# The FFN input projections of an encoder layer: block products of full depth, and seven half-depth products of block sums

## The chip, the cores and the metric

One core of a Trainium2 chip runs the kernel. The metric is the device time of one execution in microseconds (us), the median of the runs shown. The engines have short names here: PE is TensorE (matmul), PEld its weight load, DVE is VectorE, ACT is ScalarE, POOL is GpSimd and SP is SyncE, whose queue issues the DMAs. SBUF is the on-chip memory with 128 partitions, PSUM the accumulator memory of PE with eight banks of 128 x 512 float32.

## The reference, cut to what matters

The layer has 2048 tokens of width 1024. A normalised input goes through one projection, attention and a state-space mixer run side by side, an output projection is added to the residual, and then comes the FFN, which is all that the change touches. With hidden width 2816:

```python
h = rms_norm(x, norm2[i]) * (1.0 + sc2) + sh2
gt, up = jnp.split(h @ w_ffn_in[i], 2, axis=-1)
x = x + g2 * ((jax.nn.silu(gt) * up) @ w_ffn_out[i])
...
return rms_norm(x, final_norm)
```

## The kernel before

The program is written with tile pools. A scheduler puts the instructions of each engine in an order of its own, and each engine then follows its order: an instruction that waits holds up all that stands behind it on its engine. A pool gives a name a fixed number of buffers, and a new tile waits until its buffer has been read for the last time. All DMAs of the FFN stand in SP's queue, in one order too.

**Precision.** Every float32 operand of a large matmul is split in two parts of the fast type fp32r: `hi` is a cast (ACT), `lo` the operand minus `hi` (DVE or POOL). A product is three matmuls per 128 rows of depth: hi by hi, lo by hi, hi by lo.

**Stage 3** (`mix_tile`, `out_tile`, L989 to L1042) takes the tokens in 16 tiles of 128. `out_tile` makes the output projection in two PSUM halves, multiplies them by a gate into `tm` (DVE, L1025), adds them to the residual row tile `xt` (POOL, L1026), stores it to `x2_d` in DRAM, squares and sums it (ACT, L1030), and POOL makes the factor of the norm (L1032, L1033), a column of `rs2`, which stays in SBUF.

**FFN.** There are four blocks of 512 tokens. `ffn_prep(b)` (L1072) loads four row tiles `x2n`, scales them by `rs2` (ACT, L1079), transposes them on PE into PSUM tiles `ps_t4` (L1084), applies gain and shift (DVE, L1086, into `tf`), and splits the result into `ht` (ACT L1087, DVE or POOL L1088). `ffn_in` (L1091) takes the hidden columns in 22 steps f of 128. A step loads the gate's and the up half's weights [1024 x 128] (`weight`, L1062: DMA, ACT cast L1068, DVE or POOL difference L1069), and makes two sums of 24 matmuls of 128 x 128 by 128 x 512 (L1102), each in a PSUM bank of its own. Tanh (ACT) and two DVE operations that read PSUM give `th`, and ACT and POOL split it into `act`, which stays in SBUF (L1106 to L1110). `ffn_out` (L1113) makes one half of the output columns: 22 x 4 x 3 matmuls into the four banks `ps_f` (L1134 to L1136). It is called twice for a block, and the next block's `ffn_prep` stands between the two calls. `last_norm` (L1142) makes the final norm and stores the rows.

PSUM has separate pools there: two banks for the transposes, two for `ps_h`, four for `ps_f`, of which `ffn_in` borrows two in every other step.

Of the kernel before, what the change touches and what calls it, by code (L numbers as in the profile page):

```python
# [17 lines left out]
P = 128  # L18
D = 1024
# [29 lines left out]
W3A = 5  # L49
FH = 2816  # L50
# [14 lines left out]
def tile_encoder(ctx: ExitStack, tc: tile.TileContext, I, O, stop=None, dbg=None):  # L65
# [27 lines left out]
    x2_d = [dram([P, 4, D], f"x2_d{b}") for b in range(4)]  # L93
    bt_d = dram([NGC, P, GC * 2 * P], "bt_d")
# [54 lines left out]
    with ExitStack() as p1:  # L149
# [15 lines left out]
        # ---- tables of the SSM  # L165
# [26 lines left out]
        def expand(ch, eng=V):  # L192
            """state-in, state-out and in-chunk tables of GC groups"""
# [16 lines left out]
            # re: cre*are - cim*aim; minus im: ncim*are - cre*aim  # L210
# [19 lines left out]
            # impulse responses within a chunk; columns: forward only | backward only | both  # L230
# [25 lines left out]
        # ---- conditioning vector and the columns of the small parameters  # L256
# [18 lines left out]
        def row_of(i):  # L275
            """selects row i of nr for all partitions"""
# [4 lines left out]
        def ada_chunk(c0, w, tag="ad"):  # L281
            """columns c0 to c0 + w of c_act @ w_ada"""
# [70 lines left out]
        def modulate(tf, src, ht, ks, eng):  # L353
            """hi and lo parts of the modulated rows, transposed"""
# [15 lines left out]
        def ssm_setup():  # L370
            # ---- SSM parameters
# [16 lines left out]
            # dt = exp(log_dt)  # L388
# [6 lines left out]
            # exp(lr * dt) - 1 through tanh  # L395
# [7 lines left out]
            # angle reduced to [-pi, pi]  # L403
# [30 lines left out]
            # powers 0..8  # L434
# [12 lines left out]
            # unit rotor of 8 steps (backward: conjugate) and its doublings, renormalised; decay of 8 steps  # L447
# [10 lines left out]
            # directional power tables  # L458
# [8 lines left out]
            # the state input is turned back by one chunk: pbd = pb0 * e^{-i phi}, where phi is 8 steps  # L467
            # in the direction of time; un holds e^{i phi} forward and its conjugate backward
# [7 lines left out]
        def ssm_setup2(kre, kim):  # L476
# [21 lines left out]
            # Bbar = k * b  # L498
# [7 lines left out]
        # the first tiles advance with the weights  # L506
# [20 lines left out]
        def in_main(s, ht, ta, begun):  # L527
# [8 lines left out]
            def norm_rope(src, i, n):  # L536
                """heads of src, rotated, and their reciprocal norms"""
# [50 lines left out]
        def rotors(chunks, eng, tags):  # L588
            """e^{i phi m} over the half chunks"""
# [35 lines left out]
    # ------------------------------------------------------------------ attention and SSM  # L625
# [5 lines left out]
    with ExitStack() as p2:  # L631
# [30 lines left out]
        def prep_k(g, first):  # L662
            """keys as split parts: the high part of the first head, or the rest"""
# [15 lines left out]
        def prep_q(u):  # L679
            """queries of a block for a pair of heads, as split parts"""  # L680
# [20 lines left out]
        def prep_max(u):  # L701
            """minus the row maxima, as a row of the second operand"""
# [105 lines left out]
        def advance(u, n):  # L808
            """up to n steps of the preparation, not beyond unit u + 2; the steps of unit u before it starts"""
# [4 lines left out]
        def ssm_chunk(c):  # L814
            """GC groups"""
# [120 lines left out]
    # ------------------------------------------------------------------ GLU, output projection, residual  # L936
    rs2 = const([P, S], "rs2")
    with ExitStack() as p3:
# [33 lines left out]
        def split_t(src, n, dst):  # L972
            """transposes of [tokens, n * P] to hi and lo parts"""
# [15 lines left out]
        def mix_tile(s):  # L989
            """normalised mixer outputs of a tile, transposed and split"""  # L990
# [15 lines left out]
            # the SSM half is 4 times its value  # L1006
# [10 lines left out]
        def out_tile(s, mt):  # L1017
# [15 lines left out]
            GP.tensor_tensor(rs2[:, s:s + 1], r2, mhalf[:, 0:1], op=ALU.pow)  # L1033
# [15 lines left out]
    # ------------------------------------------------------------------ FFN  # L1049
    ps_h = ctx.enter_context(tc.tile_pool(name="ps_h", bufs=1, space=PSUM, reuse_waits="tile"))  # L1050
    ps_t = ctx.enter_context(tc.tile_pool(name="ps_t4", bufs=2, space=PSUM, reuse_waits="tile"))
    ps_f = ctx.enter_context(tc.tile_pool(name="ps_f", bufs=1, space=PSUM, reuse_waits="tile"))
    h4 = ctx.enter_context(tc.tile_pool(name="h4", bufs=1, reuse_waits="tile"))
    w4 = ctx.enter_context(tc.tile_pool(name="w4", bufs=3, reuse_waits="tile"))
    a4 = ctx.enter_context(tc.tile_pool(name="a4", bufs=1, reuse_waits="tile"))
    t4 = ctx.enter_context(tc.tile_pool(name="t4", bufs=2, reuse_waits="tile"))
    g2b = a4.tile([P, D], F32, tag="g2b", name="g2b")
    fnb = a4.tile([P, D], F32, tag="fnb", name="fnb")
# [3 lines left out]
    def weight(src, n, cnt):  # L1062
        """[P, n, m] of weights as hi and lo parts"""
        raw = w4.tile([P, n, src.shape[2]], F32, tag="raw", name="w_raw")
        dma(raw, src)
        hi = w4.tile([P, n, src.shape[2]], F32R, tag="whi", name="w_hi")
        lo = w4.tile([P, n, src.shape[2]], F32R, tag="wlo", name="w_lo")
        A.copy(hi, raw)  # L1068
        (GP if cnt % 4 == 3 else V).tensor_sub(lo, raw, hi)  # L1069
        return hi, lo  # L1070

    def ffn_prep(b):  # L1072
        """transposed, modulated rows of a block as hi and lo parts"""
        ht = h4.tile([P, 2, KD, 512], F32R, tag="ht4", name="ht4")
        xs = []
        for j in range(4):
            xt = h4.tile([P, D], F32, tag="x2n", name="x2n", bufs=4)
            dma(xt, x2_d[b][:, j, :])
            A.activation(xt, xt, AF.Copy, scale=rs2[:, 4 * b + j:4 * b + j + 1])  # L1079
            xs.append(xt)  # L1080
        for k in range(KD):
            pt = ps_t.tile([P, 512], F32, tag="t4", name="ps_t4")
            for j in range(4):
                T.transpose(pt[:, P * j:P * (j + 1)], xs[j][:, P * k:P * (k + 1)], ident)  # L1084
            tf = h4.tile([P, 512], F32, tag="tf", name="tf", bufs=2)
            V.tensor_scalar(tf, pt, gain2[:, k:k + 1], modc[:, 24 + k:25 + k], op0=MUL, op1=ADD)  # L1086
            A.copy(ht[:, 0, k], tf)  # L1087
            (GP if b == 0 and k % 2 else V).tensor_sub(ht[:, 1, k], tf, ht[:, 0, k])  # L1088
        return ht

    def ffn_in(ht):  # L1091
        act = [a4.tile([P, KF, 512], F32R, tag=f"act{i}", name=f"act{i}") for i in range(2)]
        for f in range(KF):
            ph = []
            for i, c0 in enumerate((P * f, FH + P * f)):
                hi, lo = weight(wfi[:, :, c0:c0 + P], KD, i)
# [113 lines left out]
```

## Time and profile before

| | |
|---|---|
| three runs | 3050.66, 3050.98, 3051.86 us, median 3050.98 |
| the profiled execution | span 3050.2 us |
| PE, DVE, POOL, ACT busy, share of the span | 95%, 52%, 42%, 38% |
| moved by DMA | 292.24 MB, mean 96 GB/s |
| the FFN in it | from 1583 us to the end |

The profiled execution's own time is its span, from the first to the last event that was recorded; it is 0.8 us below the median of the runs. A row of a view has the line of the program, the engine and the operation, what it writes and reads, and a duration in us or, where it says so, in ns. A PE row of a matmul lasts longer than the distance to the next one, since matmuls are pipelined. PEclk is the granted clock of TensorE: 1.00 is 2.4 GHz and 0.50 is 1.2 GHz, and a mean between them is a stretch with both.

### The profile page before, as it was taken

What the parts mean: (1) busy time and instruction counts of PE and PEld (TensorE: products, weight loads), DVE (VectorE), ACT (ScalarE), POOL (GpSimd) and SP (SyncE); (2) the same over time, 40 slices, a digit from 0 to 9 for tenths busy, and PEclk for the clock granted to TensorE, in tenths of its full rate; (3) what the DMA queues carried; (4) which work ended last, traced back from release to release, by engine and by line L of the source; (5) the groups of instructions that cost most, each with busy time, mean ns of one, the idle gap of its engine ahead of it and who ended that gap; (6) DMA issues with size and microseconds to landing.
All of it is one profiled execution on the core that took longest, in us unless ns stands there. A gap on an engine that the chain in (4) does not pass through costs nothing.

```text
span 3050.2 us, 36157 instructions
## 1 busy us (share of the span) xinstructions
PE 2901.0 (95%) x13548; PEld 2129.6 (70%) x13548; DVE 1598.9 (52%) x2271; ACT 1156.6 (38%) x2227; POOL 1279.9 (42%) x1062
## 2 busy tenths in 40 slices
PE   6998978889889999999999999999999999999998
PEld 4776835445445455458878888888888888888887
DVE  6879886777887755653343333433334332343323
ACT  3654544444444445452333222322223222232222
POOL 3647568778888977433231111211112111121112
PEclk7999998989999999999999999999999999999999
DMA  7764221111110100022254332533334332243322
GB/s 211 216 221 152 86 69 41 49 45 49 45 45 25 56 11 11 4 90 83 87 173 124 97 97 93 178 98 97 98 122 152 97 97 97 91 153 97 98 98 80
DMA packets 331648, 292.24 MB, mean 96 GB/s; under 512 B 44024, under 2 KB 278224, under 8 KB 330448
## 3 DMA queue, kind: packets, MB, share of 16 engines
q1 hardware_dynamic: 331472, 289.92, 30.0%
q8 instruction: 107, 1.75, 0.2%
q14 instruction: 69, 0.57, 0.1%
HBM read 243.24 MB, written 46.64 MB: 95 GB/s over the span
## 4 chain that ended last, share of the span: by engine, by line
PE 69%; DVE 4%; issue 1%; POOL 1%; ACT 1%; DVEq 0%; POOLq 0%; ACTq 0%
PE ps_h L1102 31%; PE ps_y L986 6%; PE ps_f L1134 5%; PE ps_f L1135 5%; PE ps_f L1136 5%; PE ps_o L770 4%; PE ps_st L784 2%; PE ps_s L712 2%; PE ps_st L785 2%; PE ps_z L986 2%; DVE xs L876 1%; DVE xs L875 1%; DVE mx L713 1%; DVE ys L128 1%; PE ps_t L977 1%
## 5 line engine op out<-in xcount | busy, mean ns | idle before, releaser
L1102 PE MATMUL ps_h<-ht,w_hi 128*128 128x512 f32 x2816 | 869.4, 390 | 2.3 <-DVE ht L1088 2.3
L1069 DVE TENSOR_TENSOR w_lo<-w_raw,w_hi 128x1024 fp32r<-128x1024 f32 x248 | 305.9, 1234 | 680.8 <-ACT w_hi L1068 680.6
L1068 ACT CAST w_hi<-w_raw 128x1024 fp32r<-128x1024 f32 x264 | 277.9, 1053 | 983.8 <-issue 628.8
L1102 PEld LDWEIGHTS ps_h<-ht,w_hi 128*128 128x128 f32 x2816 | 528.9, 188 | 112.2 <-DVE ht L1088 2.6
L1102 PE MATMUL ps_h<-ht,w_lo 128*128 128x512 f32 x1408 | 548.5, 390 | 0.4 <-DVE w_lo L1069 0.4
L1110 POOL TENSOR_TENSOR act<-th,act 128x512 fp32r<-128x512 f32 x88 | 157.1, 1786 | 775.9 <-ACT act L1109 775.9
L713 DVE TENSOR_REDUCE mx<-ps_s 128x1 f32<-128x512 f32 x512 | 333.1, 682 | 107.7 <-PE ps_s L712 105.6
L1102 PEld LDWEIGHTS ps_h<-ht,w_lo 128*128 128x128 f32 x1408 | 264.8, 188 | 55.8 <-DVE w_lo L1069 0.8
L1135 PE MATMUL ps_f<-w_hi,act 128*128 128x512 f32 x704 | 274.2, 389 | 0.0
L1136 PE MATMUL ps_f<-w_lo,act 128*128 128x512 f32 x704 | 273.9, 390 | 0.0
L1134 PE MATMUL ps_f<-w_hi,act 128*128 128x512 f32 x704 | 273.8, 390 | 0.0
L712 PE MATMUL ps_s<-ka,qa 128*128 128x512 f32 x512 | 211.6, 454 | 48.3 <-DVE mx L713 46.9
L368 PE MATMUL ps_z<-whi,ht 128*128 128x512 f32 (+1 forms) x768 | 226.9, 379 | 15.0 <-ACT ht L357 11.0
L784 PE MATMUL ps_st<-qa,ka 128*128 128x512 f32 x512 | 224.9, 439 | 14.9 <-ACT e__6941 L787 2.5
L712 PEld LDWEIGHTS ps_s<-ka,qa 128*128 128x128 f32 x512 | 93.6, 192 | 189.0 <-DVE mx L713 133.2
L785 PE MATMUL ps_st<-qb,kb 128*128 128x512 f32 x512 | 208.3, 407 | 0.1
L986 PE MATMUL ps_y<-wo,mt 128*128 128x512 f32 x768 | 186.2, 394 | 1.2 <-DVE on L751 0.9
L1108 DVE SCALAR_TENSOR_TENSOR th<-th,ps_h 128x512 f32<-128x512 f32 x88 | 60.5, 687 | 227.0 <-PE ps_h L1102 226.8
L368 PEld LDWEIGHTS ps_z<-whi,ht 128*128 128x128 f32 x768 | 141.1, 199 | 44.8 <-ACT ht L357 12.8
L784 PEld LDWEIGHTS ps_st<-qa,ka 128*128 128x128 f32 x512 | 98.9, 193 | 102.7 <-issue 21.7
L986 PEld LDWEIGHTS ps_y<-wo,mt 128*128 128x128 f32 x768 | 142.1, 188 | 35.3 <-DVE mt L980 4.7
L1135 PEld LDWEIGHTS ps_f<-w_hi,act 128*128 128x128 f32 x704 | 132.2, 188 | 27.3
(2266 smaller groups left out, 5041.5 us busy)
## 6 DMA issues: line engine op xcount, KB each, us to landing
w_raw<-in_w_ffn_in_dram SPq DMA_DIRECT2D x176, 512.0 KB
w_raw<-in_w_ffn_out_dram SPq DMA_DIRECT2D x88, 512.0 KB
wa<-in_w_ada_dram SPq DMA_DIRECT2D x48, 512.0 KB
xt<-in_x_dram SPq DMA_DIRECT2D x32, 512.0 KB
rot_d<-rot SPq DMA_DIRECT2D x16, 512.0 KB
rotl<-rot_d SPq DMA_DIRECT2D x8, 1024.0 KB
x_d<-xt SPq DMA_DIRECT2D x16, 512.0 KB
x2n<-x_d SPq DMA_DIRECT2D x16, 512.0 KB
```

The source lines that it names most:

```text
L368: T.matmul(pp[:, 0:c1 - c0], ht[:, a, k], w[:, k, c0:c1], start=k == 0 and j == 0, stop=k == KD - 1 and j == 2)
L712: T.matmul(p1_, qa[h][:, P * j:P * (j + 1)], ka[kv][f], start=True, stop=True)
L713: red = V.reduce_max(mx[:, 4 * h + j, f:f + 1], p1_, axis=AX.X)
L784: T.matmul(st_, ka[kv][k // 4][:, ks], qa[h], start=True, stop=False)
L785: T.matmul(st_, kb[kv][k // 4][:, ks], qb[h], start=False, stop=True)
L986: T.matmul(out, lhs[:, a, k], rhs[w][k][:, cs_], start=n == 0, stop=n == last)
L1068: A.copy(hi, raw)
L1069: (GP if cnt % 4 == 3 else V).tensor_sub(lo, raw, hi)
L1102: T.matmul(pp, w[:, k], ht[:, a, k], start=n == 0, stop=n == 23)
L1134: T.matmul(pf[j], act[0][:, f, js], hi[:, e], start=f == 0, stop=False)
L1135: T.matmul(pf[j], act[1][:, f, js], hi[:, e], start=False, stop=False)
L1136: T.matmul(pf[j], act[0][:, f, js], lo[:, e], start=False, stop=f == KF - 1)
```

## The change

Tokens are now taken in two halves of 1024. Depth (1024 rows of the weights) is cut in two halves of 512, the tokens of a half in two groups of 512, and the hidden columns of a step f in gate and up. That is a 2 x 2 by 2 x 2 block product, and it is made with seven block products of depth 512 in place of eight, by sums of blocks (`s1` and the like on the weights, `t1` to `t4_` on the activations). Sums and differences are made in float32 before the split in hi and lo.

- `out_tile` also scales its row tile by the norm's factor (`xn`, ACT) and stores it to DRAM (`xn_d`). `xn` takes the only buffer of the name `tm`.
- `ffn_prep(t)` handles a half in four parts kk. It loads two depth tiles of 128 as `xk` (one buffer), transposes them into four PSUM banks, and makes seven operands `xc0` to `xc6` [128 x 512], each with hi and lo. They stay in 28 buffers.
- `ffn_in(t, xc)` has 22 steps of seven products `prod` with 12 matmuls. Three banks `ps_ha`, `ps_hb`, `ps_hc` serve a step. A partial sum is copied out of the bank (`r1`, `r2`, `r3`, ACT) and the accumulation goes on in it. `th` is split and stored to DRAM (`act_d`).
- `ffn_out(b, last)` makes both halves of the columns at once in eight banks. It reads the activations back (`act_i`, 512 KB per f) into the buffers of `xc`, and the weights as two [128 x 512] tiles. `finish_rows` loads the residual rows, adds, normalises and stores.
- All eight PSUM banks are one name of one pool.

```diff
+NTMP = 10
+NHL = 14
+NRAW = 8
...
+            rs2 = t3.tile([P, 1], F32, tag="rs2", name="rs2")
+            GP.tensor_tensor(rs2, r2, mhalf[:, 0:1], op=ALU.pow)
+            xn = t3.tile([P, D], F32, tag="tm", name="xn", bufs=1)
+            A.activation(xn, xt, AF.Copy, scale=rs2)
+            dma(xn_d[s // 8][:, s % 8, :], xn)
...
+    def bank(name):
+        return ps_a.tile([P, 512], F32, tag="acc", name=name, bufs=8)
+    def slot(i, kk, name, dt=F32R):
+        return xc4.tile([P, 2, 512], dt, tag=f"xc{i}{kk}", name=name)
+    def split(src, eng):
+        hi, lo = half("w_hi"), half("w_lo")
+        A.copy(hi, src)
+        eng.tensor_sub(lo, src, hi)
...
+    def ffn_prep(t):
+        xc = [[None] * KH for _ in range(7)]
+        for kk in range(KH):
+            xk = w4.tile([P, 8, 2, P], F32, tag="xk", name="xk", bufs=1)
+            for i in range(2):
+                k = kk + KH * i
+                dma(xk[:, :, i], xn_d[t][:, :, P * k:P * (k + 1)])
+            for i in range(2):
+                for h in range(2):
+                    pt = bank("ps_t4")
+                    for j in range(4):
+                        T.transpose(pt[:, P * j:P * (j + 1)], xk[:, 4 * h + j, i], ident)
+                    B[i][h] = tmp(f"tf{i}{h}")
+                    V.tensor_scalar(B[i][h], pt, gain2[:, k:k + 1], modc[:, 24 + k:25 + k], op0=MUL, op1=ADD)
+            tt(t1, B[0][1], B[0][0], SUB)
+            tt(t2, B[1][1], t1, SUB)
+            tt(t4_, B[1][0], t2, SUB, GP)
+            tt(t3_, B[1][1], B[0][1], SUB, GP)
+            for i, src in ((0, B[0][0]), (4, t1), (5, t2), (1, B[1][0]), (6, t3_), (3, t4_), (2, B[1][1])):
+                x = slot(i, kk, f"xc{i}")
+                A.copy(x[:, 0], src)
+                tt(x[:, 1], src, x[:, 0], SUB, GP if i in (2, 6) else V)
...
-            for i, c0 in enumerate((P * f, FH + P * f)):
-                hi, lo = weight(wfi[:, :, c0:c0 + P], KD, i)
-                for k in range(KD):
-                    for (w, a) in ((hi, 0), (hi, 1), (lo, 0)):
-                        T.matmul(pp, w[:, k], ht[:, a, k], start=n == 0, stop=n == 23)
...
+            a11, a12, a21, a22 = raw
+            def prod(out, w, i, first, last):
+                hi, lo = w
+                for kk in range(KH):
+                    for n, (l, a) in enumerate(((hi, 0), (hi, 1), (lo, 0))):
+                        T.matmul(out, l[:, kk], xc[i][kk][:, a], ...)
+            pa, pb, pc = bank("ps_ha"), bank("ps_hb"), bank("ps_hc")
+            prod(pa, split(a11, V), 0, True, True)
+            A.copy(r1, pa)
+            tt(s1, a21, a22, ADD, GP)
+            prod(pb, split(s1, V), 4, True, True)
+            tt(a21, a11, a21, SUB, GP)
+            tt(s1, s1, a11, SUB)
+            prod(pa, split(s1, V), 5, False, True)
+            A.copy(r2, pa)
+            prod(pc, split(a12, V), 1, True, True)
+            tt(a12, a12, s1, SUB)
+            V.tensor_tensor(c0_, pc, r1, op=ADD)
+            A.activation(th, c0_, AF.Tanh, scale=0.5)
+            V.scalar_tensor_tensor(th, th, 1.0, c0_, op0=ADD, op1=MUL)
+            prod(pa, split(a21, V), 6, False, True)
+            A.copy(r3, pa)
+            V.tensor_tensor(up1, pb, r3, op=ADD)
+            prod(pa, split(a22, V), 3, False, True)
+            V.scalar_tensor_tensor(th, th, 0.5, pa, op0=MUL, op1=MUL)
+            store(2 * t, f, th)
+            prod(pb, split(a12, V), 2, False, True)
+            V.tensor_tensor(c1_, pb, r2, op=ADD)
...
+            store(2 * t + 1, f, th)
...
+    def ffn_out(b, last):
+        pf = [[bank(f"ps_f{j}{h}") for h in range(2)] for j in range(4)]
+        cut = KF - TAIL
...
+                n = f % 16
+                ai = slot(n % 7, 3 - n // 7, "act_i")
+                dma(ai.bitcast(F32), act_d[b][:, f])
...
+    def finish_rows(s, pf, last):
+        xr = slot(2 + s % 4, 1, "x2r", F32).rearrange("q h d -> q (h d)")
...
+    ffn_in(0, xc)
+    ffn_out(0, False)
+    ffn_out(1, False)
+    xc = ffn_prep(1)
+    ffn_in(1, xc)
+    ffn_out(2, False)
+    ffn_out(3, True)
```

PE's order inside `ffn_in`. Before, two sums follow each other, and each has a bank of its own (`ps_h` with its buffer's number):

```order
L1102 MATMUL ps_h_14317<-ht4_13647,w_hi_14313 128x512 x2
L1102 MATMUL ps_h_14317<-ht4_13647,w_lo_14314 128x512
L1102 MATMUL ps_h_14354<-ht4_13647,w_hi_14350 128x512 x2
L1102 MATMUL ps_h_14354<-ht4_13647,w_lo_14351 128x512
```

Now, where the products with `xc5`, `xc6` and `xc3` of one step meet (ps_ha_14114 is that step's first bank, ps_ha_14426 the one of two steps later):

```order
L1131 MATMUL ps_ha_14114<-xc5_13930,w_lo_14155 128x512
L1131 MATMUL ps_ha_14114<-xc6_13756,w_hi_14194 128x512 x2
...
L1131 MATMUL ps_ha_14114<-xc6_13936,w_lo_14195 128x512
L1131 MATMUL ps_ha_14426<-xc0_13744,w_hi_14429 128x512 x2
L1131 MATMUL ps_ha_14114<-xc3_13759,w_hi_14214 128x512 x2
```

The three products go into one bank, and between them ACT's copies `r2` and `r3` read it. Nothing stands between the first two, two matmuls of a later step between the second and the third.

ACT's order where stage 3 ends. Before (`jk3` is the square of a row tile, the second one that of the last tile):

```order
L1030 ACTIVATE jk3_13545,ss2_13546<-xt3_13488 128x1024
L1079 ACTIVATE x2n_13648<-x2n_13648,rs2_11662 128x1024
...
L1068 CAST w_hi_13738<-w_raw_13736 128x1024
L1068 CAST w_hi_13769<-w_raw_13767 128x1024
L1087 CAST ht4_13647<-tf_13665 128x512
L1068 CAST w_hi_13806<-w_raw_13804 128x1024
L1087 CAST ht4_13647<-tf_13674 128x512
L1030 ACTIVATE jk3_13608,ss2_13609<-xt3_13551 128x1024
```

Now, from the square of the last tile on:

```order
L1034 ACTIVATE jk3_13673,ss2_13674<-xt3_13616 128x1024
L1040 ACTIVATE xn_13680<-xt3_13616,rs2_13678 128x1024
L1081 CAST w_hi_13961<-w_raw_13949 128x512
L1081 CAST w_hi_13980<-w_sum_13957 128x512
L1081 CAST w_hi_13998<-w_sum_13957 128x512
L1081 CAST w_hi_14016<-w_raw_13951 128x512
L1110 CAST xc0_13744<-tf00_13713 128x512
```

The last tile's square and its scaled copy stood behind the FFN's first casts or were not there; now they stand ahead of all of them.

SP's order where the first `ffn_in` ends. Before, only weights are loaded there (`w_raw`, 512 KB each). Now (`act_i_17465` is the tile of f = 2, `x2r` a residual row tile of 512 KB, `act_o` an output of the last steps):

```order
L1206 DMA x2r_18210<-x2_d0_75 128x1024
L1185 DMA act_i_17769<-act_d0_81 128x1024
L1185 DMA act_i_17503<-act_d0_81 128x1024
L1206 DMA x2r_18171<-x2_d0_75 128x1024
L1189 DMA wo_raw_17625<-in_w_ffn_out_dram 128x512
L1185 DMA act_i_17731<-act_d0_81 128x1024
L1185 DMA act_i_17465<-act_d0_81 128x1024
L1173 DMA act_d0_81<-act_o_17351 128x1024
```

The load for the third f of `ffn_out` stands behind thirteen other loads of activations, since its buffer is the operand of the last product of `ffn_in`.

## Rows read from the trace of the kernel before

**Rows 1.** The page, part 1: busy us, share of the span, instructions.
```profile
PE 2901.0 (95%) x13548; PEld 2129.6 (70%) x13548; DVE 1598.9 (52%) x2271; ACT 1156.6 (38%) x2227; POOL 1279.9 (42%) x1062
```

**Rows 2.** Chain of waits, FFN: start us, us, engine, tile, line, count.
```profile
1956.12 0.87 PE ps_t L1084 x8
1957.00 239.38 PE ps_h L1102 x1056
```

**Rows 3.** Windows: length, busy PE PEld DVE ACT POOL, PEclk, DMA share, GB/s.
```profile
800.00:1100.00 300.00, 271.50 (x1117) 145.22 (x1117) 228.92 (x261) 137.69 (x244) 251.96 (x169) 0.93 0.13 37
1580.00:1600.00 20.00, 16.98 (x79) 13.41 (x78) 13.17 (x14) 7.19 (x11) 8.55 (x6) 0.91 0.85 284
2705.00:2945.00 240.00, 240.00 (x1061) 198.79 (x1060) 78.69 (x84) 66.58 (x84) 40.12 (x22) 1.00 0.33 99
```

**Rows 4.** Group by line, FFN: busy us, mean ns, idle before.
```profile
L1135 PE MATMUL ps_f<-w_hi,act 128*128 128x512 f32 x704 | 274.2, 389 | 0.0
```

**Rows 5.** Timeline: PE, an ACT copy of its bank, PE again; restart.
```profile
1340.99 1.53 PE L736 MATMUL ps_rs<-acc,ones 128*32 128x512 f32 x4 [1.85 <-DVE acc L732]
1342.56 0.58 ACT L739 COPY acc<-ps_rs 64x512 f32<-64x512 f32 x1 [0.43 <-PE ps_rs L736]
1343.19 0.69 PE L743 MATMUL ps_rt<-ident,acc 64*128 64x64 f32 x4
...
1589.57 0.50 PE L1102 MATMUL ps_h<-ht,w_hi 128*128 128x512 f32 x1 [2.33 <-DVE ht L1088]
1589.91 0.40 PE L1102 MATMUL ps_h<-ht,w_lo 128*128 128x512 f32 x1
```

**Rows 6.** Single lines: count, duration in ns as minimum, median, maximum.
```profile
L730 ACT COPY ot<-ps_o x16: 569/587/641, 453.2 to 1341.5; 128x512 f32<-128x512 f32 x16
L1087 ACT CAST ht<-tf x32: 609/620/626, 1585.1 to 2633.5; 128x512 fp32r<-128x512 f32 x32
L1086 DVE TENSOR_SCALAR tf<-ps_t,gain,modc x32: 798/804/811, 1584.3 to 2631.9; 128x512 f32<-128x512 f32 x32
L1088 DVE TENSOR_TENSOR ht<-tf,ht x28: 677/686/2475, 1587.8 to 2634.8; 128x512 fp32r<-128x512 f32 x28
```

**Rows 7.** Timeline: DVE beside POOL, without and with two SBUF inputs.
```profile
1890.64 3.79 POOL L1121 TENSOR_TENSOR x2r<-x2r,ty 128x512 f32<-128x512 f32 x3 [26.67 <-DVE ty L1120]
1892.02 0.69 DVE L1120 TENSOR_TENSOR ty<-ps_f,g2b 128x512 f32<-128x512 f32 x1 [0.74 <-POOL x2r L1121]
...
1901.99 2.40 POOL L1069 TENSOR_TENSOR w_lo<-w_raw,w_hi 128x1024 fp32r<-128x1024 f32 x1 [5.78 <-ACT w_hi L1068]
1902.46 2.47 DVE L1088 TENSOR_TENSOR ht<-tf,ht 128x512 fp32r<-128x512 f32 x1 [0.93 <-ACT ht L1087]
```

**Rows 8.** Timeline where stage 3 ends: last tiles' residual and norm.
```profile
1574.27 1.06 ACT L1030 ACTIVATE jk<-xt 128x1024 bf16<-128x1024 f32 x1 [1.69 <-POOL xt L1026]
1575.78 0.55 POOL L1033 TENSOR_TENSOR rs<-r,mhalf 128x1 f32<-128x1 f32 x1
1583.43 1.03 PE L1084 MATMUL ps_t<-ident,x2n 128*128 128x128 f32 x8
1584.39 2.37 POOL L1026 TENSOR_TENSOR xt<-xt,tm 128x1024 f32<-128x1024 f32 x1 [8.07 <-DVE tm L1025]
```

**Rows 9.** Windows of one stretch, L1102 alone, then L1084 alone.
```profile
1583.40:1616.26 32.86, 26.55 (x99) 19.22 (x100) 0.95 0.75 259
1583.40:1616.26 32.86, 5.65 (x38) 4.46 (x37) 0.95 0.75 259
```

**Rows 10.** Timeline: a DMA and its first reader; `tm` in steady stage 3.
```profile
1601.17 1.75 SPq L1078 DMA_DIRECT2D x2n<-x_d  x4
1605.35 2.43 ACT L1079 ACTIVATE x2n<-x2n,rs 128x1024 f32<-128x1024 f32 x2 [2.30 <-DMA x2n<-x_d]
...
1514.38 0.55 POOL L1033 TENSOR_TENSOR rs<-r,mhalf 128x1 f32<-128x1 f32 x1
1521.79 0.68 DVE L1025 TENSOR_TENSOR tm<-ps_y,g1b 128x512 f32<-128x512 f32 x1
```

More of the change, by code (lines that the diff above doesn't have):

```diff
@@ L934, in tile_encoder @@
         return
-    rs2 = const([P, S], "rs2")
     with ExitStack() as p3:
@@ L1047, in tile_encoder @@
         return
[L1050 to L1055, printed above, removed]
+    ps_a = ctx.enter_context(tc.tile_pool(name="ps_a", bufs=1, space=PSUM, reuse_waits="tile"))
@@ L1072, in ffn_prep @@
[L1072 to L1080, printed above, removed]
-        for k in range(KD):
[L1082 to L1089, printed above, removed]
@@ L1113, in ffn_out @@
-    def ffn_out(act, h, xrs, last=False):
-        hs_ = slice(512 * h, 512 * h + 512)
-        pf = [ps_f.tile([P, 512], F32, tag=f"f{j}", name=f"ps_f{j}") for j in range(4)]
-        def add(j):
-            tf = t4.tile([P, 512], F32, tag="th", name="ty")
-            V.tensor_tensor(tf, pf[j], g2b[:, hs_], op=MUL)
-            (V if last else GP).tensor_tensor(xrs[j][:, hs_], xrs[j][:, hs_], tf, op=ADD)
-        n = KF // 2
-        cut = n - TAIL if last else n
-        held = {}
-        steps = [(f2, j) for f2 in range(cut) for j in range(4)] + [(f2, j) for j in range(4) for f2 in range(cut, n)]
-        for f2, j in steps:
-            if f2 not in held:
-                held[f2] = weight(wfo[:, 2 * f2:2 * f2 + 2, hs_], 2, f2)
-            hi, lo = held[f2]
-            js = slice(P * j, P * (j + 1))
-            for e in range(2):
-                f = 2 * f2 + e
-                T.matmul(pf[j], act[0][:, f, js], hi[:, e], start=f == 0, stop=False)
-                T.matmul(pf[j], act[1][:, f, js], hi[:, e], start=False, stop=False)
-                T.matmul(pf[j], act[0][:, f, js], lo[:, e], start=False, stop=f == KF - 1)
-            if f2 == n - 1:
-                add(j)
-                if last:
-                    last_norm(12 + j, xrs[j])
@@ new lines, in store @@
+    def store(b, f, th):
+        ao = t4.tile([P, 2, 512], F32R, tag="ao", name="act_o", bufs=2)
+        A.copy(ao[:, 0], th)
+        GP.tensor_sub(ao[:, 1], th, ao[:, 0])
+        dma(act_d[b][:, f], ao.bitcast(F32))
+    def ffn_out(b, last):
+        pf = [[bank(f"ps_f{j}{h}") for h in range(2)] for j in range(4)]
+        cut = KF - TAIL
+        held = {}
+        steps = [(f, j) for f in range(cut) for j in range(4)] + [(f, j) for j in range(4) for f in range(cut, KF)]
+        for f, j in steps:
+            if f not in held:
+                n = f % 16
+                ai = slot(n % 7, 3 - n // 7, "act_i")
+                dma(ai.bitcast(F32), act_d[b][:, f])
+                ws = []
+                for h in range(2):
+                    r = w4.tile([P, 512], F32, tag="wr", name="wo_raw", bufs=NRAW)
+                    dma(r, wfo[:, f, 512 * h:512 * h + 512])
+                    hi, lo = half("wo_hi"), half("wo_lo")
+                    A.copy(hi, r)
+                    (GP if f % 4 == 3 else V).tensor_sub(lo, r, hi)
+                    ws.append((hi, lo))
+                held[f] = ai, ws
+            ai, ws = held[f]
+            js = slice(P * j, P * (j + 1))
+            for h in range(2):
+                hi, lo = ws[h]
+                for n, (a, w) in enumerate(((0, hi), (1, hi), (0, lo))):
+                    T.matmul(pf[j][h], ai[:, a, js], w, start=f == 0 and n == 0, stop=f == KF - 1 and n == 2)
+            if f == KF - 1:
+                finish_rows(4 * b + j, pf[j], last)
```

94 lines of the change are left out of this document (47 added, 47 removed).

## The prediction

> **What bounds the kernel now.** The busy times of the page come first: PE is busy for 95% of the span, DVE for half of it, POOL and ACT for less [rows 1]. Then the chain of waits, to see what PE's share is made of in the FFN. The reader is to see one piece of 1056 matmuls that lasts 239.38 us without a wait, which is one block's `ffn_in`; two later blocks have such a piece too, and between them stand `ffn_out`'s matmuls with groups of eight transposes of 0.87 us [rows 2]. A matmul costs 239.38 / 1056 = 0.2267 us and a transpose 0.109 us. The windows agree: from 2705 to 2945 us PE is busy for the whole stretch at a granted clock of 1.00, DVE for 79 of 240 us, ACT for 67, POOL for 40, and the DMA engines for 33% [rows 3]. So the FFN costs as many times 0.2267 us as it has matmuls. A matmul that goes is worth its full price, as long as PE still never waits. That condition is where the change has to be judged.
>
> **What goes.** `ffn_in` has 4 x 1056 = 4224 matmuls. Now it has 2 halves x 22 steps x 7 products x 12 = 3696. 528 x 0.2267 = 119.7 us less. `ffn_out` keeps 3 x 704 [rows 4], and the 128 transposes of the four blocks stay.
>
> **Waits inside a step.** The order of PE shows `xc5`, `xc6` and `xc3` of one step in one bank, with ACT's copy between. The nearest rows are PE, a copy of its bank, PE: PE ends at 1340.99 + 1.53 = 1342.52, the copy starts 0.04 us later and ends at 1343.14, and PE goes on 0.05 us after it [rows 5]. A copy of the full 128 x 512 takes 0.587 us [rows 6]. The last matmul of a product is recorded with 0.39 us [rows 4], 0.163 more than the distance to a next one, and the first after a wait holds up its successor for 0.34 instead of 0.23 us [rows 5]. So the first of the two places costs 0.163 + 0.04 + 0.587 + 0.05 + 0.11 = 0.95 us. At the second place two matmuls of a later step fill 0.45 of it: 0.50 us. 1.45 x 44 steps = 64 us. Below: the second is filled and the restart is free, 0.84 x 44 = 37. Above: one copy stands behind an ACT cast of 0.62 us [rows 6], 2.07 x 44 = 91. I take 64, since the nearest rows give it term by term. The rest of a step I cost at nothing: it needs 14 ACT operations of some 0.6 us, 16 of DVE of 0.6 to 0.7 and 4 of POOL of 1.3, beside 19 us of matmuls that cover them.
>
> **The two preparations.** Before, the preparation of three blocks lay between two calls of `ffn_out`, with no wait of PE [rows 2]. Now `ffn_out` holds all eight banks, so the transposes of the second half start after its last matmul, and everything behind them is open. A part kk needs of DVE four evictions of 0.804 us and seven operations with two SBUF inputs of 0.686 us [rows 6], 3.2 + 4.8 = 8.0 us, and of POOL four operations of 3.79 / 3 = 1.26 us [rows 7], 5.1 us. They don't run side by side freely. A DVE operation with a PSUM input keeps its 0.69 us beside POOL, but one with two SBUF inputs that started at 1902.46 ended at 1904.93, 0.54 us behind POOL's end at 1904.39 [rows 7]: nearly all of its work came after POOL's. POOL can use the evictions' 3.2 us; I let half of its time fall on the others: 10.6 us for a part.
>
> First half: ACT's order has the last tile's square and its scaled copy ahead of all FFN casts. From PE's last output matmul (T, 1583.4) that is 0.7 us of `tm`, 2.37 of POOL [rows 8], 2.06 from the square's start to the norm's factor [rows 8], and a copy of 1.06: T + 6.4. Three casts and differences of weights stand ahead of the first eviction: T + 9. The first part with the other weight operations takes some 11.5 us, three more 10.6 each: T + 52. Until then PE has 64 transposes and the 55 matmuls that stand ahead of the last part's operands, 7.0 + 12.5 = 19.5 us; it loses 32.5. The same stretch before lost 32.86 - 99 x 0.2267 - 38 x 0.109 = 6.3 [rows 9]. Net +26. Second half: no such copy, but the last rows' norm (4.4 us of DVE, 2.5 of POOL) and eight weight operations put the first part's end at T + 19, the last at T + 51: +31. Below, with DVE alone and nothing ahead, 35 us less the same PE work: +9 and +16. Above, with POOL never beside DVE (13.1 for a part): +36 and +42. I take the values between, as the rows show both kinds of neighbours.
>
> **Activations back from DRAM.** An f of `ffn_out` now moves 1.05 MB in 24 x 0.2267 = 5.44 us, 193 GB/s; the 284 GB/s of one stretch [rows 3] cover it. Where `ffn_in` ends they don't: a buffer of `xc` comes free only when the last product has read it. In the last 12 us SP's order releases eight loads of activations, three of rows and three of weights, 6.5 MB. At 284 GB/s that takes 23 us, so the load for the third f lands some 11.5 us after the last product, when 2.7 us of matmuls are left: 9 us of wait, twice, +18. Below 0 (it all fits), above 40 (half the rate).
>
> By the Trainium skill ("DMA: Bandwidth & Descriptors", Measured) a long load stream reaches 425 GB/s on a core alone. At that figure an estimate for the 6.5 MB is 15.4 us, the wait would be 1.5 us, and the sum below 15 us less. No row here is above 284 GB/s; the sum goes by that.
>
> **Small terms.** After a wait of PE the granted clock falls: 0.91 over 20 us [rows 3], where 1.8 us are lost. Four such places, +8 (0 to 15). In stage 3 `xn` takes `tm`'s buffer: factor at 1514.93, copy 1.06, store as long as a load, 4.2 us [rows 10], is 1520.2, and `tm` is written at 1521.79. Hidden by 1.6 us; if not, up to +10. The end has one output half more to evict and add in the last rows, 2 x 0.69: +1.4.
>
> **Sum.** -119.7 + 64 + 26 + 31 + 18 + 8 + 1.4 = +29 us. The profiled execution's span is 3050.2, and with the 0.8 us by which the median is above it I forecast 3080 us. With likely errors of 20 us on the step's waits and 20 on the preparations its own range is 3045 to 3115.
>
> **Rivals.**
> Waits that stay small: the products go, and the second place is filled, the preparations cost what DVE alone needs, the loads arrive in time. -119.7 + 37 + 9 + 16 + 0 + 4 + 1.4 = -52, 2999 us at the end of all lower bounds; with half of each distance to my values it is 3040, and the typical case is 3020. For it: PE is the only engine near its limit [rows 1], and DVE is idle for two thirds of the FFN. Against: the rows of the copy leave no room below 0.84 us. It decides from waits and preparations below 119.7 us together. Chance 0.26 for faster by more than 0.2%.
>
> The clock turns down in `ffn_in`: PE now stops twice in each step. From 800 to 1100 us PE was busy for 90.5% with many short stops, and the granted clock was 0.93 [rows 3]; a step is busy for 19.05 of 20.5 us, 93%. At a clock of 0.93, 44 x 20.5 = 902 us become 970: +68 on my sum, 3148 us. Against: the stops of that stretch were of several us. Chance 0.08. The Trainium skill ("TensorE: Matmul & The Clock Gate", A second HAM failure mode: psum-queue depth-cycling) describes such short idles between groups of matmuls that cycle through PSUM banks, and a clock that swings between 1.2 and 2.4 GHz by them; it gives no price, and rows 3 are the nearest case here.
>
> The DMA queue doesn't hold 193 GB/s through `ffn_out`, as loads wait in SP's one order behind buffers and stores. It decides from a rate below 193 GB/s; at nine tenths of that each of 88 f takes 6.04 instead of 5.44 us, +53, 3133 us. For it: the profile has no long stretch of such a rate. Against: 284 GB/s was reached over 20 us [rows 3]. Chance 0.06.
>
> **How the numbers follow.** What a measurement of this kernel can tell from no change is about 0.2%, 6 us. My forecast has 0.54, the two slower rivals 0.14: slower 0.68. Faster has 0.26, and 0.06 lies within 0.2%, where small waits and my terms meet. The range leaves out 0.1 at each end: from 3010, inside the fast rival, to 3130, near the DMA rival.
>
> **What would show it.** In the profile after, `prod`'s line should have 3696 matmuls and idle time of PE before them released by ACT's copies, close to 1.45 us x 44. Windows of 84 matmuls should last 20.5 us. Behind stage 3 and in the middle of the FFN there should be two stretches of some 50 us with PE busy for less than half, and DVE's differences in them longer than 0.69 us where POOL runs. At each end of `ffn_in` PE should wait some 9 us for `act_i`. If a step lasts 19.1 us, the waits' term is wrong; if PE is through a preparation in 30 us, the share of POOL is; a granted clock below 0.97 inside `ffn_in` speaks for the clock rival, and waits for DMA spread over `ffn_out` for the DMA rival.

## The result, and the profile after

The changed kernel takes 3100.77 us, the median of four runs (3099.46 to 3104.61), beside 3050.82 us for the kernel before: a ratio of 1.0169, 95% interval 1.0154 to 1.0183. It is 50 us slower. The forecast was 3080 us with a range of 3010 to 3130.

The page of the changed kernel, part 1, answers to [rows 1]. PE is busy for 78 us less, but its share falls from 95% to 91%, since the span grew by 48.6 us to 3098.8.

```profile
PE 2823.2 (91%) x13020; PEld 2032.2 (66%) x13020; DVE 1920.2 (62%) x2719; ACT 1272.6 (41%) x2603; POOL 1475.7 (48%) x1198
```

The chain of waits in the FFN (start us, us, engine, tile, line, count) answers to [rows 2]. Before, one piece of 1056 matmuls ran for 239.38 us. Now a step is a row of pieces with stops between them (the longer ones stand here). From 2544.59 to 2565.73 is one step, 21.14 us, while its 84 matmuls need 84 x 0.2267 = 19.04. The last two lines are the end of the second `ffn_in`: a load in the chain, and then `ffn_out` in one unbroken piece.

```profile
2544.59 2.81 PE ps_ha L1131 x11
2548.09 5.79 PE ps_ha L1131 x24
2553.88 5.44 PE ps_hb L1131 x24
2559.32 2.72 PE ps_hc L1131 x12
2565.73 2.80 PE ps_ha L1131 x11
...
2849.09 8.99 DMA act_i<-act_d
2858.13 226.01 PE ps_f L1200 x987
```

PE's waits from 1575 us on (what waited, for what: us in total, times, longest us) name four releasers: the copy of `r2` (first line), the rows of a preparation, a cast of weights (third line, at the second stop of a step), and the reloads of activations.

```profile
PE ps_ha L1131 <- ACT r L1144: 38.7, 40, 1.0
PE ps_t L1100 <- DMA xk<-xn_d: 29.8, 6, 9.4
PE ps_ha L1131 <- ACT w_hi L1081: 19.9, 42, 0.5
PE ps_f L1200 <- DMA act_i<-act_d: 12.5, 2, 6.6
```

Windows of the changed kernel (columns as in [rows 3]) show the first preparation, the second, the reload behind the first `ffn_in`, and 300 us of steady `ffn_in`. In the steady stretch the granted clock is 1.00, although PE stops twice in every step. In both preparations DVE is busy for 97% of the time, PE for 56% and 67% at a mean clock of 0.61 and 0.64. The reload moved 383 and 408 GB/s.

```profile
1590.00:1637.00 47.00, 26.25 (x93) 19.89 (x94) 45.78 (x55) 21.20 (x37) 35.22 (x19) 0.61 0.58 162
2345.00:2390.00 45.00, 30.10 (x102) 22.85 (x103) 43.82 (x53) 18.07 (x32) 32.91 (x19) 0.64 0.33 96
2098.00:2106.00 8.00, 2.51 (x12) 1.74 (x10) 4.71 (x6) 3.55 (x7) 4.54 (x3) 0.92 1.00 383
2106.00:2113.00 7.00, 6.59 (x18) 5.21 (x19) 0.00 (x0) 0.00 (x0) 0.00 (x0) 0.61 1.04 408
...
2440.00:2740.00 300.00, 279.22 (x1193) 220.19 (x1193) 195.54 (x227) 115.83 (x198) 93.81 (x56) 1.00 0.32 100
```

The timeline at the two stops of a step (start us, us, engine, line) answers to [rows 5]. The last matmul of `xc5` ends at 2543.62. The copy of `r2` starts only at 2543.95, because a cast of weights stands ahead of it on ACT, and that cast started at 2543.43, when PE gave a weight buffer back. The same happens at the second place: a cast at 2547.42, and behind it the copy of `r3`. There the two matmuls that fill the wait need that very cast, so they start 0.48 us late. Counted from start to start of PE's matmuls, every step in two stretches of 300 us loses 1.24 us at the first place and 0.78 at the second.

```profile
2543.23 0.39 PE L1131 MATMUL ps_ha<-xc,w_lo 128*128 128x512 f32 x1
2543.43 0.62 ACT L1081 CAST w_hi<-w_raw 128x512 fp32r<-128x512 f32 x1 [2.05 <-PE ps_ha L1131]
2543.95 0.58 ACT L1144 COPY r<-ps_ha 128x512 f32<-128x512 f32 x1
...
2544.59 0.73 PE L1131 MATMUL ps_ha<-xc,w_hi 128*128 128x512 f32 x2 [0.97 <-ACT r L1144]
...
2547.42 0.62 ACT L1081 CAST w_hi<-w_raw 128x512 fp32r<-128x512 f32 x1 [2.35 <-PE ps_ha L1131]
2547.94 0.58 ACT L1154 COPY r<-ps_ha 128x512 f32<-128x512 f32 x1
...
2548.09 0.74 PE L1131 MATMUL ps_ha<-xc,w_hi 128*128 128x512 f32 x2 [0.48 <-ACT w_hi L1081]
```

### The profile page after: what moved, and what is told of

It reads as the page before. It is cut to its first block, busy times and chain, and to the rows that moved or that the text cites. A ratio compares the mean times of both kernels' runs of the same rounds, so it can differ in the third digit from the quotient of the medians.

```text
span 3098.8 us, 37226 instructions
## 1 busy us (share of the span) xinstructions
PE 2823.2 (91%) x13020; PEld 2032.2 (66%) x13020; DVE 1920.2 (62%) x2719; ACT 1272.6 (41%) x2603; POOL 1475.7 (48%) x1198
## 5 line engine op out<-in xcount | busy, mean ns | idle before, releaser
L1131 PE MATMUL ps_ha<-xc,w_hi 128*128 128x512 f32 x1408 | 445.3, 402 | 62.2 <-ACT r L1144 38.7
L1200 PE MATMUL ps_f<-wo_hi,act_i 128*128 128x512 f32 x1408 | 434.5, 392 | 14.4 <-DMA act_i<-act_d 12.5
L1172 POOL TENSOR_TENSOR act_o<-th,act_o 128x512 fp32r<-128x512 f32 x88 | 149.6, 1700 | 486.4 <-ACT act_o L1171 486.4
L1131 PEld LDWEIGHTS ps_ha<-xc,w_hi 128*128 128x128 f32 x1408 | 257.4, 190 | 154.4 <-ACT r L1144 55.6
L1200 PEld LDWEIGHTS ps_f<-wo_hi,act_i 128*128 128x128 f32 x1408 | 266.1, 189 | 72.4 <-DMA act_i<-act_d 13.3
L1082 DVE TENSOR_TENSOR w_lo<-w_raw,w_hi 128x512 fp32r<-128x512 f32 x220 | 235.1, 1082 | 113.5 <-ACT w_hi L1081 113.5
L1200 PE MATMUL ps_f<-wo_lo,act_i 128*128 128x512 f32 x704 | 272.2, 391 | 0.0
L1131 PE MATMUL ps_ha<-xc,w_lo 128*128 128x512 f32 x704 | 270.7, 394 | 0.0
L1081 ACT CAST w_hi<-w_raw 128x512 fp32r<-128x512 f32 x220 | 136.2, 620 | 315.3 <-PE ps_ha L1131 177.3
L1131 PE MATMUL ps_hb<-xc,w_hi 128*128 128x512 f32 x704 | 218.3, 390 | 0.0
```

Source lines behind the costliest of these rows:

```text
L1081: A.copy(hi, src)
L1082: eng.tensor_sub(lo, src, hi)
L1131: T.matmul(out, l[:, kk], xc[i][kk][:, a], start=first and kk == 0 and n == 0, stop=last and kk == KH - 1 and n == 2, skip_group_check=True)
L1172: GP.tensor_sub(ao[:, 1], th, ao[:, 0])
L1200: T.matmul(pf[j][h], ai[:, a, js], w, start=f == 0 and n == 0, stop=f == KF - 1 and n == 2)
```

## The experiments

Theory A, for the steps: PE stops because three products in succession share a bank, and each copy stands behind a cast. Its rival B: the weight casts are late, and the bank is beside the point. For the preparations, theory P says that DVE (with POOL on the same way to SBUF) sets their length, and theory D that the loads of the rows do. All runs are compared with the changed kernel's 3101 us.

**One cast behind the copy.** In the same step:

```diff
-            A.copy(r2, pa)
+            cp = A.copy(r2, pa)
...
-            prod(pb, split(a12, V), 2, False, True)
+            with tc.issue_after(cp.ins):      # queued behind it on its engine
+                w = split(a12, V)
+            prod(pb, w, 2, False, True)
```

> Edit: ACT's cast of the weights of xc2 is queued behind the copy of r2 in the same step; PE's order then has 20 matmuls of the next step's xc0 and xc4 between xc6 and xc3, and nothing between xc5 and xc6. Theory A (PE stops because xc5, xc6 and xc3 share a bank, and each copy stands behind a cast that itself waits for PE): the second stop is filled, the first costs what the rows of the copy say, 0.95 us, in place of the 2.06 us per step of the changed kernel (21.10 minus 84 x 0.2267). 1.1 x 44 = 48 us less: 3052 us. Theory B (the weight casts come late because their buffers and differences do; the bank is beside the point): a step stays at 21.1 us, 3101 us, with PE's idle time released by the casts of w_hi.

Measured: 3053.59 us, and a step of 20.01 us. The timeline of this kernel shows the stop that is left. PE's last matmul ends at 2506.71, the copy starts 0.03 us later, and PE goes on 0.06 us after its end. The stop costs 20.01 - 19.04 = 0.97 us; the prediction had 0.95 for just this case. PE's order changed with ACT's: matmuls of other banks now stand between `xc6` and `xc3`, and no stop is left there. Theory A holds for the step as a whole. B has a part in it: at the second place of the changed kernel it is the cast that PE waits for last (0.48 us, the third line of PE's waits above). Whether more weight buffers, so that the cast need not wait for PE, would do as much was not tried.

```profile
2506.32 0.39 PE L1131 MATMUL ps_ha<-xc,w_lo 128*128 128x512 f32 x1
2506.74 0.58 ACT L1144 COPY r<-ps_ha 128x512 f32<-128x512 f32 x1 [2.39 <-PE ps_ha L1131]
...
2507.38 0.50 PE L1131 MATMUL ps_ha<-xc,w_hi 128*128 128x512 f32 x1 [0.68 <-ACT r L1144]
```

**`xc1` between `xc5` and `xc6`.** The first matmul of each product is pinned behind what the program has before it on PE:

```diff
-                        T.matmul(out, l[:, kk], ...)
+                        mm = T.matmul(out, l[:, kk], ...)
+                        if kk == 0 and n == 0:
+                            tc.keep_in_program_order(mm)
```

> Edit: the first matmul of each product is pinned behind the product before it in the program, so xc1 (another bank) stands between xc5 and xc6, and xc3 follows xc6 with nothing between. Theory A: the first stop is gone, the second is whole; 0.95 us if the copy of r3 starts at PE's end, 1.56 if it stands behind a cast of 0.62 us as ACT's order has it. A step of 20.0 to 20.6 us, 3053 to 3079 us; I expect 3079. Theory B: 21.1 us, 3101 us.

Measured: 3080.17 us, a step of 20.43 us. The first stop is gone; the second, with nothing in it, costs 20.43 - 19.04 = 1.39 us. The timeline of ACT has the reason: the copy of `r3` (L1156 here) starts 0.53 us behind the cast that stands ahead of it.

```profile
2506.67 0.62 ACT L1081 CAST w_hi<-w_raw 128x512 fp32r<-128x512 f32 x1 [1.21 <-PE ps_ha L1131]
2507.20 0.58 ACT L1156 COPY r<-ps_ha 128x512 f32<-128x512 f32 x1
```

**A product between every two of one bank.** As above, and the step is split so that the next step's `xc0` comes ahead of `xc3`:

```diff
+        for f in range(KF):
+            next(cur)                        # xc4, xc5, xc1, xc6 of step f
+            if nxt: next(nxt)                # xc0 of step f + 1
+            next(cur, None)                  # xc3, xc2 of step f
```

> Edit: as the pinned order, and the program is written so that the next step's xc0 stands between xc6 and xc3; each of the three products in one bank then has 12 matmuls (2.72 us) of another bank before its successor. Theory A: a copy behind a cast needs 1.56 us and is covered at both places, no stop is left: 84 x 0.2267 = 19.05 us per step, 2.06 x 44 = 90 us less than 3101: 3010 us. Theory B: the casts stay late, 21.1 us a step, 3101 us.

Measured: 3017.51 us, 83 us less, and below the kernel before: ratio 0.9895 (0.9881 to 0.9910). The window of 300 us has no idle time of PE left, and the step is 19.04 us. The 7 us that are missing lie in the preparations. Up to 1667 us PE lost 38.9 us in the changed kernel, some 3 of them at stops of the first steps; here it lost 39.3 without one. In the second preparation it is 35.3 and 37.6. With the products pinned, PE takes nothing of the later ones while an operand of the first is missing; that this is the whole reason was not shown.

```profile
2440.00:2740.00 300.00, 300.00 (x1325) 248.43 (x1324) 187.90 (x253) 129.48 (x222) 88.65 (x61) 1.00 0.35 114
```

**Other buffers for the activations.**

```diff
-                ai = slot(n % 7, 3 - n // 7, "act_i")
+                ai = slot((0, 4, 1, 5)[n // 4], n % 4, "act_i")
...
-        xr = slot(2 + s % 4, 1, "x2r", F32)
+        xr = slot(6, s % 4, "x2r", F32)
```

> Edit: the loads of activations in ffn_out go into the buffers of xc0, xc4, xc1 and xc5 (four columns each), which PE is through with before the last products, and the rows of x2 into those of xc6; before, the third load waited for a buffer that the last product reads. Theory A (the wait of 8.3 and 9.0 us at the two ends of ffn_in is that one load's, begun too late): both waits vanish, and the half clock behind them (2 x 6.8 us, 3.4 us lost each): 24 us less, 3077 us. Theory B (the volume is the limit: 6.5 MB at 284 GB/s take 23 us wherever they begin): 0 to 8 us less, 3093 to 3101 us.

Measured: 3080.81 us, 20 us less, near theory A's 24; B falls. This kernel's waits of PE from 2060 to 2330 us have no load of activations any more; over the end of each `ffn_in` and the first 27 us of `ffn_out` PE loses 2.9 us each time in place of 12.0 and 12.1, the half clock included.

```profile
PE ps_ha L1131 <- ACT r L1144: 1.0, 1, 1.0
PE ps_f L1200 <- ACT wo_hi L1191: 1.0, 2, 0.5
```

**Rows loaded ahead.** Three of a preparation's four parts get row buffers of their own, those of the operands that are made last:

```diff
+                if kk:                       # parts in the order 1, 2, 3, 0
+                    x = xc4.tile([P, 8, P], F32, tag=f"xc{2 * kk - 2 + i}0", name="xk")
+                else:
+                    x = w4.tile([P, 8, P], F32, tag="xk", name="xk", bufs=2)
```

> Edit: the rows xk of three of the four parts of a preparation have buffers of their own (those of the part that is prepared last), so that their loads don't wait for the transposes of the part before. Theory D (the loads of xk set the length of the preparations: PE waits 20.5 us for them in the first one, 9.4 in the second, which I had not foreseen): both go, 15 to 30 us less than 3101: 3071 to 3086 us. Theory P (DVE and POOL set it, as predicted; DVE has work without a pause from 1590 to 1640 us, and the loads lie in its shade): 0 to 8 us less, 3093 to 3101 us, and PE's waits move to DVE's evictions. I expect 3093, a part of the second preparation's.

Measured: 3103.55 us, nothing gained (ratio to the kernel before 1.0173, 1.0158 to 1.0188). The waits for `xk` are nearly gone in the first preparation, 1.9 us are left, but PE's waits of this kernel up to 1660 us show where they went: to DVE's evictions, which themselves stand behind a weight that now loads behind all the rows. PE loses 43.4 us there in place of 38.9, so the first preparation doesn't price the rows alone.

```profile
PE ps_ha L1137 <- DVE tf L1108: 10.3, 1, 10.3
PE ps_t L1106 <- DMA w_raw<-in_w_ffn_in_dram: 10.3, 1, 10.3
PE ps_t L1106 <- DVE tf L1108: 5.5, 1, 5.5
PE ps_t L1106 <- DMA xk<-xn_d: 1.9, 2, 1.2
```

The second one does. No weight is late in it, and PE's longest waits from 2260 to 2420 us are for DVE's evictions; none for `xk` is left, where the changed kernel had 9.1 us of them. PE loses 35.3 us in both kernels. Theory P holds there, and D falls.

```profile
PE ps_t L1106 <- DVE tf L1108: 11.9, 3, 9.4
PE ps_ha L1137 <- DVE tf L1108: 6.1, 1, 6.1
```

**No POOL in the preparations** (rows not ahead; `GP` becomes `V` in `ffn_prep`):

> Edit: POOL's four operations in each part of a preparation go to DVE. Theory P (the two engines hold each other up over SBUF inputs): 16 operations more per preparation at 0.60 us are 9.6 us more for DVE, but its operations beside POOL, 1.72 us each, fall to 0.60, and POOL's of 5 to 6 us are gone from the chain; 3 to 6 us less per preparation: 3089 to 3095 us. Rival (POOL works beside DVE at no cost, the long operations are waits for something else): DVE's load grows by 2 x 9.6 us: 3115 to 3120 us.

Measured: 3097.61 us. The 3 us are half of the least that was expected and inside the uncertainty of the comparison. What it excludes is the rival: 32 operations more on DVE, 19 us at 0.60, cost nothing. In the first 57 us of the two preparations together DVE is busy for 105.0 us with 125 operations in the changed kernel, and for 105.4 us with 160 in this one, so POOL's part of the work had held DVE up by about as much.

**Rows ahead, no POOL, half of the evictions on ACT** (`A.activation(..., AF.Identity, bias=..., scale=...)` for i = 1):

> Edit: rows loaded ahead, POOL's operations on DVE, and two of a part's four evictions on ACT. Theory P: DVE's need per preparation falls from 48 us to 8 evictions x 0.73 + 44 operations x 0.60 + 12 of the weights x 0.60 = 39.5 us, and nothing else is late: 8.5 x 2 = 17 us less, and some of the loads' part: 3080 us (3075 to 3085). Theory D: what the rows loaded ahead give by themselves, and no more.

Measured: 3096.52 us, a miss by 16. In the second preparation PE loses 30.8 us in place of 35.3, about half of the 8.5 expected. In the first it loses 39.6, no less than before, and the timeline of this kernel's DVE gives the reason: it does its work in 41 us, near the 39.5 reckoned, but starts at 1598.32: first in its order is the difference of a weight, whose load stood behind 4 MB of rows.

```profile
1583.19 0.69 DVE L1030 TENSOR_TENSOR tm<-ps_y,g1b 128x512 f32<-128x512 f32 x1 [2.14 <-PE ps_y L991]
1598.32 0.69 DVE L1083 TENSOR_TENSOR w_lo<-w_raw,w_hi 128x512 fp32r<-128x512 f32 x1 [14.44 <-ACT w_hi L1082]
```

**All together**, with twelve early buffers for the activations, the loads of the second half's rows held back until the second `ffn_out`, and the second half's first part put ahead of that `ffn_out`'s last rows.

> Edit: all of it together (products of another bank between those of one bank, early buffers for the activations, rows loaded ahead, no POOL in the preparations, half of the evictions on ACT), and the second preparation's first part is put ahead of ffn_out's last rows. If the terms add up: 3101 - 90 for the stops in the steps - 24 for the reloads and their half clock - 20 for the two preparations - 8 for the early part = 2960 us; if the preparations give nothing, 2987 us. I expect 2970 us, below the kernel before by 80 us. Against it speaks only that the loads of rows, weights and activations may meet at the ends of ffn_in.

Measured: 3005.89 us, 36 us more than expected. From 1650 to 2280 us and from 2350 to 2990 PE is busy all the time, so the stops and the reloads are gone; what is left lies in the preparations. The first lost 45.5 us, against 38.9 in the changed kernel: DVE starts late, as in the run before. The pinned order keeps PE from later products as well; its share was not measured by itself. The second lost 35.3.

**DVE first.** The first step's weights load behind the first part's rows; their casts and differences are queued behind the first part's operands:

```diff
+        with tc.issue_after(behind[0]), tc.issue_after(behind[1]):
             next(cur)
```

> Edit against e8_all: the first step's weights are loaded behind the first part's rows and ahead of the other rows, and their casts and differences stand behind the first part's operands on ACT and DVE. In the kernels with the rows loaded ahead DVE's first operation of the first preparation is the difference of a weight that lands only at 1597.7 us; DVE has 41 us of work from there. Theory P (a preparation lasts as long as DVE's work from the moment it can start): it starts 8 to 13 us earlier in the first preparation and 2 to 4 in the second, 10 to 15 us less than e8_all's 3006: 2993 us. Rival (PE's order, with all 64 transposes ahead of the products, or ACT behind the last output tile, sets it): 3003 to 3007 us.

Measured: 2991.30 us, as theory P had it. DVE's first eviction of this kernel (first line) starts 11.5 us earlier than in the run before (second line), and the loss in the first preparation is 34.2 us, 11.3 less.

```profile
1585.97 1.52 DVE L1130 TENSOR_SCALAR tf<-ps_t,gain,modc 128x512 f32<-128x512 f32 x2
...
1597.49 1.52 DVE L1114 TENSOR_SCALAR tf<-ps_t,gain,modc 128x512 f32<-128x512 f32 x2
```

**The first two steps not pinned, evictions of three parts on ACT:**

> Edit against e9_dve_first: the products of the first two steps of each half are not pinned, so that PE can take what is ready of three products while the last parts are prepared; ACT makes all evictions of the last three parts, DVE those of the first. Theory P: DVE's need falls by 12 x 0.73 - 8 x 0.73 = 3 us per preparation, and some 40 matmuls of the first steps (9 us) fall into the wait for the last part: 10 us less per half at most, 2975 to 2985 us. Rival: the evictions on ACT queue behind its casts, and it becomes the bound of a part (4 x 0.67 + 7 x 0.52 + casts of weights, against 6.6 us of DVE): 2990 us or more.

Measured: 2977.61 us, a ratio of 0.9765 (0.9748 to 0.9781) to the kernel before. The losses in the two preparations are 27.2 and 24.4 us. The time is in the expected range; which of the two changes did how much was not tried apart.

**Sums of weights from POOL to DVE** in those steps (`GP if f >= NP else V`):

> Edit against e10_best: in the first two steps of each half the sum and the difference of weights go from POOL to DVE (four operations of 0.60 us more for DVE per half). In e10_best POOL's sum for the second step lasts 13.64 us in the first preparation and 11.91 in the second, beside DVE's operations with two SBUF inputs, where it takes 1.26 us alone, and the chain runs through it. Theory P (the two engines share the way to SBUF, and POOL stands still while DVE works without a pause): the operation lasts 0.69 us on DVE, and the chain moves to DVE's own work, which is 2.4 us longer; 3 to 8 us less per half where PE waits for that step's products: 2962 to 2972 us. Rival (POOL's record is only a rough span, PE waits for the last part's operands in any case): 2976 to 2982 us.

Measured: 2976.38 us, no difference; the rival holds. In the run before this one POOL's operation (shown at the end) was as long as its record says, since ACT's cast starts 0.03 us behind it (first line), but PE's wait for that cast was only 3.01 us (second line). With the sum on DVE, PE waits in smaller pieces for the last part's operands, as long in total: over the whole FFN it loses 51.6 us before and 50.2 with it.

```profile
1617.28 0.62 ACT L1084 CAST w_hi<-w_sum 128x512 fp32r<-128x512 f32 x1 [3.06 <-POOL w_sum L136]
1617.95 0.73 PE L1159 MATMUL ps_hb<-xc,w_hi 128*128 128x512 f32 x2 [3.01 <-ACT w_hi L1084]
```

## Why the prediction was right, and which term was not

The forecast of slower held, 21 us short. The FFN gives the account. After, it lasts 1505.9 us from the first transpose to the last matmul; 5808 matmuls x 0.2267 and 128 transposes x 0.109 are 1330.6 of it, so 175.3 us are lost. Before, 6.6 were.

- **What goes**, -119.7: as said. A matmul kept its 0.2267 us: the window without stops has 1325 of them in 300 us.
- **Waits inside a step**, 64 predicted. This is the term that was mis-sized: a step loses 21.10 - 19.04 = 2.06 us, 2.06 x 44 = 90.6. The first place lost 1.24 us where 0.95 was said, the second 0.78 where 0.50 was said. I had taken the value without a cast, by rows in which nothing stood ahead of the copy. Those rows priced their own case well: with the cast out of the way the stop was 0.97 us. But ACT's order has the cast ahead of the copy in every step, and the cast waits for a buffer that PE frees at the end of the same product. At the first place the copy starts 0.33 us behind PE's last matmul instead of 0.03; at the second the two matmuls that were to fill the wait need the cast themselves. In the pinned order, where the cast begins later, it costs 1.39 - 0.97 = 0.42 at one stop. The upper bound of the prediction, 2.07, had a copy behind a cast; that it meets 2.06 is luck, since it put a whole cast of 0.62 us on one copy, and the trace has some 0.3 at each of the two places. The order could have told that; the typical case was not the nearest rows' case.
- **Preparations**, 32.5 + 31 lost, and some 4 of the clock's 8. Of the 98.3 us lost in the two preparations and the two reloads, some 13 are stops of the 6.2 steps in them (44 less two stretches of 398.4 / 21.1), and 20 the reloads, 24.1 less two steps' stops: some 65 are left. The size was right, and so was the start: the first eviction was predicted 9 us behind the last output matmul, whose end is at 1582.84 in this trace, and came at 1592.62. That the one buffer of `xk` would show as a wait of PE, 29.8 us in all, I had not foreseen; the second preparation of the run with rows ahead shows that it cost nothing there by itself. For the first, that it lay in the shade of DVE's work is argued from DVE's 97%, not shown.
- **Activations back from DRAM**, 18 predicted, and 4 of the clock: the two ends lost 20 together, and the run with other buffers gained 20, of which the traces show 18 at these places. PE stood still for 5.9 and 6.6 us (12.5 in its waits above), where 9 were said. The 8.27 and 8.99 us in the chain are the load itself, and PE still had 2.4 us of matmuls when it began. The reason was right, a load that begins behind the last product, and the rate was too low: what was to land behind that product, 11.5 us at 284 GB/s, is 3.3 MB, and at the 383 GB/s of the window it takes an estimated 8.5 us. The Trainium skill's figure ("DMA: Bandwidth & Descriptors", Measured), 425 GB/s, is nearer: 383 and 408 were reached. By that figure the wait would have been an estimated 1.5 us; it was longer: in the 12 us ahead of the last product's end, when buffers come free one by one, the queue moved only 310 and 320 GB/s.
- **Clock**: in the FFN the half clock appears in and behind the preparations and the reloads only. The rival by which it turns down inside `ffn_in` fell: 1.00 over 300 us with two stops in each step. The rival of the DMA rate fell too: `ffn_out` runs for 226 us without a wait. The queue moves only 164 to 179 GB/s in it, as part of its tiles were loaded before; in the run with all together it moved 222 GB/s over 220 us without a wait of PE. Stage 3 stayed as it was (the first transpose starts at 1582.84, before at 1583.43), and the end is 0.3 us longer, not 1.4.
- **Waits that stay small**, the rival on the other side, 0.26: it can be made true by an edit of the order alone (3017.51 us), but this program's order doesn't do it.

## What to carry to other kernels

When products accumulate in one bank with a copy between them, another bank's product has to stand between them in PE's order, and what stands ahead of the copy on its engine counts with it: here the stops of a step took 2.06 us, and the one stop that was left without the cast 0.97. An algorithm that saves an eighth of the matmuls of `ffn_in` lost 50 us with one order of PE and gained 33 with another; the 73 us of the best run took the early buffers and shorter preparations as well. A wait that the profile puts on a load may have no price: look at which engine is busy all through it before you buy the load off.

## What the runs showed of the hardware

POOL and DVE hold each other up on operations with two SBUF inputs, and who loses depends on the neighbours. In the first preparation of the changed kernel (timeline), a POOL operation that takes 1.26 us alone lasted 6.09 us, until DVE turned to evictions from PSUM, while DVE kept 0.69; ten microseconds later the two take turns, 1.72 and 1.75 us.

```profile
1596.63 6.09 POOL L133 TENSOR_TENSOR xc<-tf,xc 128x512 fp32r<-128x512 f32 x1 [5.80 <-ACT xc L1110]
1596.69 0.69 DVE L133 TENSOR_TENSOR tc<-tf,tf 128x512 f32<-128x512 f32 x1
...
1606.27 1.72 POOL L133 TENSOR_TENSOR tc<-tf,tf 128x512 f32<-128x512 f32 x1
...
1606.78 1.75 DVE L133 TENSOR_TENSOR xc<-tf,xc 128x512 fp32r<-128x512 f32 x1
```

In the run with the two first steps not pinned, DVE works without a pause from 1599.8 to 1616.1 us, its operations keep 0.68 us, and POOL's one sum beside them took 13.64 us (timeline of POOL):

```profile
1603.61 13.64 POOL L136 TENSOR_TENSOR w_sum<-w_raw 128x512 f32<-128x512 f32 x1 [16.94 <-ACT xc L1141]
1617.32 1.28 POOL L136 TENSOR_TENSOR w_raw<-w_raw 128x512 f32<-128x512 f32 x1
```

The Trainium skill ("Trainium Architecture — The Big Picture", What this means for kernel authors) says that of the engines only these two contend for SBUF, by an exclusive lock and not by a share of the bandwidth. The rows agree: POOL's operation lasts some twelve microseconds longer than alone while DVE's keep their length, rather than both running at half speed. Why they take turns in one stretch and not in the other was not tried.
